# A planned encoder kernel: in-place steps counted at the shared port, other landing times, and six rank points for each stage

## The chip, the cores and the metric

The kernel runs on 1 core of one Trainium2 chip. The metric is device time in microseconds from launch to end, the median of 3 runs. The profile is one further execution of the same program; its span runs from the first to the last instruction.

## What is computed

A trunk of two layers on x of 1024 tokens by 1024 features, all in float32. Each layer does this (`lax` and reshapes left out):

```python
h = rms_norm(x, norm1_g[l])
proj = h @ w_in[l]
(a_cq, a_ckv, a_kr, b_q, b_k, b_v, c_q, c_k, c_v, d_q, d_k, d_v) = jnp.split(proj, splits, axis=-1)
y_a = mla_mixer(...)    # group A: latent attention, 4 heads, dense over 1024 keys
y_b = diff_mixer(...)   # group B: differential attention, 4 heads, two softmaxes each, dense
y_c = swa_mixer(...)    # group C: banded attention, +-128 tokens, sink logits
y_d = na_mixer(...)     # group D: neighbourhood attention on the 64-wide grid, with a bias
mix = jnp.concatenate([rms_norm(y_a, out_g_mla[l]), y_b,
                       rms_norm(y_c, out_g_swa[l]), rms_norm(y_d, out_g_na[l])], axis=-1)
x = x + mix @ w_out[l]
h = rms_norm(x, norm2_g[l])
x = x + jnp.square(jax.nn.relu(h @ w_up[l])) @ w_down[l]
```

and after the last layer a final `rms_norm`.

## The kernel before

The kernel is written as a program of steps, and the order of the steps is not the order of the code. Every call such as `nc.vector.tensor_tensor(...)` goes to `Plan.add`, which records a `Step`: its engine, its operands, and the steps that it must follow. `Plan.order`, the list pass, then walks through an imagined time, picks for each engine the ready step with the lowest rank, and gives tiles their buffers. `Trunk.emit` issues the steps in the order of their imagined starts. For that reason every instruction has the same line, L696, in the profile. On the chip each engine runs its own queue in that order, and engines wait for each other only where data or a buffer asks for it; the imagined times are not enforced.

What the pass knows of the chip stands in a few places:

- `Plan.price` gives each step an occupancy and a latency, from its engine and size. For a transfer it gives 470 ns for the issue on SyncE and a time that depends on the bytes and on the length of the contiguous runs.
- `Plan.issue` moves the imagined clock. A transfer begins some time after its issue and lands a fixed time after its last byte; a consumer gets a further `LATE`. A VectorE or GpSimd step with two wide inputs in SBUF takes the shared port: it starts no sooner than the last such step of either engine has ended. An input that is the same view as the output is not in `s.ins` and so does not count as an input there.
- `s.slack` belongs to TensorE's steps. In the first of two searches a step is passed over until it has been ready for `slack` ns; only where nothing else can go does the second search take it. Matmuls and transposes that read `p` (probabilities) have a slack of their own, with another value in stage `b`.
- `SPAN` gives each stage of each layer a list of points ("knots"). `Plan.stream` spreads the stage's steps evenly over the list by TensorE cost, and the rank of a step is read off between two points. A stage whose points are lower goes first wherever both are ready. A step's rank is also lowered to that of any step that needs it.
- `Place.ROOM` caps the live buffers of each tile name; a name that is not in it has the count in the code (`bufs`, or `CAPS` by stage).

The stages of a layer: `open` (norm, first three column tiles of the input projection, and the first rotary tables), `b1`, `lat`, `pd`, `pc` (the other projections), `up` (the latent products of group A), `b`, `d`, `c`, `a` (attention by group), `mb`, `md`, `mc`, `ma` (norm and gain of the groups' outputs, split in a high and a low part, the tiles `mix`), `o1`, `o2` (output projection), and `mlp`. Attention stages overlap freely; MLP is a Strassen-like product with 16 groups of up-projection and 4 of down-projection.

Steps and tiles named below: matrix products run as three passes of fp32r parts, so operands are split: ScalarE makes the high part, VectorE or GpSimd subtracts it for the low part (`xh`/`xl`, `wh`/`wl`, `both`, `mix`). `sq` and `acc` are sums of squares, added in place. `tabc` and `tabs` are rotary tables, multiplied in place by a row of norms. `yc` and `y` are the outputs of groups, multiplied in place by `rz`, the inverse denominators. `raw` are MLP weights, combined by additions and subtractions, partly in place (`s1`, a sum of two, has two buffers in the code). `lat`, `qb`, `kb` are DRAM tensors that the kernel writes and reads back, into `latp` and `stack`. `act` are MLP activations read back. In an in-place call the code passes the same view twice:

```python
def times(self, y, rz, eng=None):
    self.tt(y, y, rz, eng=eng or self.nc.gpsimd)
```

All transfers but 96 stores of the MLP are issued by SyncE, in the planned order; a transfer whose data or buffer is not ready holds up those behind it.

Of the kernel before, what the change touches and what calls it, by code (L numbers as in the profile page):

```python
# [249 lines left out]

class Step:
    __slots__ = ("n", "eng", "op", "args", "kw", "outs", "ins", "before", "after", "rank", "unit",
                 "start", "done", "cells", "cost", "tiled", "slack")


class Unit:
# [16 lines left out]
class Plan:  # L273
# [42 lines left out]
    def add(self, q, op, args, kw):  # L316
        s = Step()
        s.n, s.eng, s.op, s.args, s.kw = len(self.steps), q, op, args, kw
        out = kw.get("out", args[0] if args else None)
        s.outs = [v for v in (out, kw.get("accum_out")) if isinstance(v, View)]  # L320
        s.ins = [v for v in chain(args, kw.values()) if isinstance(v, View) and all(v is not o for o in s.outs)]
        s.rank = self.lead
        s.unit = self.unit or Unit()
        s.unit.steps.append(s)
        s.start, s.tiled = None, False
        before = set()

        def clash(a, b):
            if not np.may_share_memory(a, b):
                return False  # L330
            if a.ndim == b.ndim == 2 and a.strides == b.strides and a.strides[1] == 4 < a.strides[0]:
                row, wide = divmod(b.ctypes.data - a.ctypes.data, a.strides[0])
                hits = lambda r, c: -b.shape[0] < r < a.shape[0] and -4 * b.shape[1] < c < 4 * a.shape[1]
                return hits(row, wide) or hits(row + 1, wide - a.strides[0])
            try:
                return np.shares_memory(a, b, max_work=4000)
            except Exception:
                return True

        def same(a, b):  # L340
            return a.shape == b.shape and a.strides == b.strides and a.ctypes.data == b.ctypes.data

        for v in s.ins:
            c = v.cell
            before.update(p for p, a in c.writes if clash(a, v.arr))
            c.reads.append((s.n, v.arr))
        for v in s.outs:
            c, whole = v.cell, v.arr.size == v.cell.arr.size
            before.update(p for p, a in chain(c.writes, c.reads) if p != s.n and clash(a, v.arr))
            if whole:  # L350
                c.writes, c.reads = [], [r for r in c.reads if r[0] == s.n]
            else:
                c.writes = [w for w in c.writes if not same(w[1], v.arr)]
                c.reads = [r for r in c.reads if r[0] == s.n or not same(r[1], v.arr)]
            c.writes.append((s.n, v.arr))
        before.discard(s.n)
        s.before, s.after = [self.steps[p] for p in before], []
        for p in s.before:
            p.after.append(s)
        s.cells = []  # L360
        for v in chain(s.outs, s.ins):
            if v.cell.kind and v.cell not in s.cells:
                s.cells.append(v.cell)
        for c in s.cells:
            c.steps.append(s)
        s.cost = self.price(s)
        s.slack = 0
        if q.name == "tensor":
            names = {v.cell.name for v in s.ins}
            s.slack = (1996 if self.stage == "b" else 248) if "p" in names else 0 if names & self.FIRM else 1996  # L370
            if names & {"rs_r", "rz", "sq", "part"} and self.stage not in ("open", "b1"):
                s.slack = 2087
        self.steps.append(s)
        return s


    def price(self, s):

        q, op = s.eng.name, s.op
        out = s.outs[0] if s.outs else None  # L380
        if op == "dma_start":
            runs = []
            for v in s.args[:2]:
                if isinstance(v, View):
                    dims = [(st // 4, n) for st, n in zip(v.arr.strides, v.arr.shape)]
                else:
                    dims = list(v.ap)
                run = 1
                for st, n in reversed(dims):
                    if n > 1:  # L390
                        if st != run:
                            break
                        run *= n
                if isinstance(v, View) and v.cell.kind and run > v.arr.shape[-1]:
                    run = min(run, math.prod(v.cell.shape[1:]))
                runs.append(run)
            size, run = 4 * max(v.arr.size for v in s.args[:2] if isinstance(v, View)), min(4 * min(runs), 4096)
            per = 12 + run / 26.5 if run >= 512 else 9 + run / 30
            return 470.0, size / run * per * 1.33 / 16
        n = math.prod(out.arr.shape[1:])  # L400
        psum = any(v.cell.kind == "bank" for v in s.ins)
        if q == "tensor":
# [10 lines left out]
        if q == "scalar":  # L413
            d = 0.832 * n + (50 if psum else 94)
# [7 lines left out]
        d = 1.04 * n + 65  # L422
# [110 lines left out]

    LOOK, HOLD = 40, {}
    FIRM = {"wh", "wl", "wah", "wal", "wkeep", "stack", "v"}
    LATE = 537

    def stuck(self, avail):
        lines = []
# [45 lines left out]
    def issue(self, s, t):  # L585

        q = s.eng.name
        s.start = t
        occ, lat = s.cost
        if s.op == "dma_start":  # L590
            lane = self.turn % 8
            self.turn += 1
            t = s.start = max(t, self.lanes[lane])
            begin = max(t + 1100, self.pipe)
            self.pipe = begin + lat
            s.done = self.pipe + (100 if any(v.cell.kind for v in s.ins) else 950)
            self.lanes[lane] = s.done + 17
            return t + occ
        if q == "tensor":
            k = int(t // 3413.33)  # L600
            while self.window < k:
                self.window += 1
                was, a = self.slow[self.window - 1], self.act.get(self.window - 1, 0.0) / 3413.33
# [9 lines left out]
            s.done = t + occ * (2 if s.tiled else 1) + 180 * (1.5 if slow else 1)  # L613
            return t + occ
        if q in ("vector", "gpsimd"):
            wide = [v for v in s.ins if math.prod(v.arr.shape[1:]) > 1]
            if len(wide) > 1 and all(v.cell.kind != "bank" for v in wide):
                t = max(t, self.port)
                self.port = t + occ
                s.start = t  # L620
# [4 lines left out]
class Place:  # L625


    def __init__(self, plan, bufs=1):
# [2 lines left out]
    CAPS = {"st": {"b": 10, "d": 8, "c": 6, "a": 12}, "p": {"b": 5, "d": 4, "c": 4, "a": 6},  # L631
            "v": {"b": 2, "d": 2, "c": 2, "a": 3}, "pt": {"b": 6, "d": 6, "c": 6, "a": 8},
            "y": {"b": 2, "d": 2, "c": 2, "a": 2}}
    ROOM = {'a4': 13, 'act10': 15, 'bias3': 2, 'big16': 19, 'cb4': 10, 'es4': 3, 'mask1': 3, 'ms2': 7,
# [5 lines left out]

    def tile(self, shape, dt, tag, bufs=None, name=None):
        n, bufs, stage = math.prod(shape[1:]), bufs or self.bufs, self.plan.stage
# [13 lines left out]
class Trunk:  # L656
# [264 lines left out]
    def attention(self, l):  # L921
# [162 lines left out]
                share(self.mm_ps(), m, 1, self.weights(w_out[m, 0]) + self.weights(w_out[m, 1]), range(8))  # L1084

    SPAN = {
        'open': ((20.62, 20.78, 85.68, 85.85), (1310.39, 1339.46, 1345.64, 1356.83)),
        'b1': ((83.39, 102.03, 186.33, 225.41), (1317.52, 1397.09, 1531.38, 1531.38)),
        'lat': ((274.83, 295.08, 308.49, 326.42), (1506.09, 1506.09, 1570.31, 1573.33)),
# [13 lines left out]
        'mlp': ((618.60, 841.24, 1010.20, 1261.11), (1855.54, 2022.97, 2217.58, 2430.52)),}  # L1103
    SOON, IDLE = 20, 12
    BANKS = {"mm": 8, "tr": 4, "sb": 2, "pv": 2}
    EARLY, NP = 4, 6
# [992 lines left out]
```

## Time and profile before

| | |
|---|---|
| median of 3 runs | 2492.53 us (2492.34 to 2497.19) |
| the profiled execution | 2490.28 us, span 2488.5 us |
| TensorE busy (matmuls) | 2445.0 us, 98% |
| VectorE busy | 1894.0 us, 76% |
| ScalarE busy | 1294.0 us, 52% |
| GpSimd busy | 379.8 us, 15% |
| mean granted TensorE clock | 0.996 |
| moved by DMA | 378.31 MB, mean 152 GB/s |

PE is TensorE, PEld its weight loads, DVE VectorE, ACT ScalarE, POOL GpSimd, SP SyncE. In rows of instructions `out<-in` names tiles, and x is the count. A row of stretches has start and end, length, the busy time of each engine with its count of instructions, then the granted TensorE clock (1.00 is full), the share of the DMA engines that is busy, and GB/s. Idle time of TensorE in a stretch is its length less PE's busy time. In the chain (the work that ended last, followed back from the end) a row is start, length, and what it is.

### The profile page before, as it was taken

The page shows a single profiled execution, that of the slowest core. Times are in us where ns is not written, and L with a number is a line of the kernel's source. Part 1 is how long each engine was busy: PE and PEld are TensorE (multiplying, and loading weights), DVE is VectorE, ACT ScalarE, POOL GpSimd, SP SyncE. Part 2 cuts the span into 40 slices and gives each one's busy share as a digit, 9 for nine tenths or more (in the row PEclk, how much of TensorE's full clock was granted, in tenths as well). Part 3 has the DMA queues.
Part 4 walks back from the last instruction along what each step waited for, and adds up shares of the span by engine and source line. Part 5 has one row for each costly group of instructions (what it writes and reads, how often), then busy time and mean ns, then how long its engine had stood idle before and what let it go on. Part 6 is the DMA issues. An engine that isn't in the chain of part 4 may idle for free.

```text
span 2488.5 us, 35364 instructions
## 1 busy us (share of the span) xinstructions
PE 2445.0 (98%) x12260; PEld 1962.3 (79%) x12260; DVE 1894.0 (76%) x3536; ACT 1294.0 (52%) x2405; POOL 379.8 (15%) x266
## 2 busy tenths in 40 slices
PE   8999999999999999999999999999999999999998
PEld 6777776777888888888877777777788888888887
DVE  7588757767877779888657786777688777897886
ACT  4466656644544445444426565676555444544454
POOL 4033324113000000000032241330330000000000
PEclk9999999999999999999999999999999999999999
DMA  5455487522244468444143645874313444774321
GB/s 188 135 165 140 124 253 231 157 83 75 98 151 154 151 219 286 137 148 144 72 140 100 176 136 144 222 235 126 109 58 127 157 150 164 248 246 153 122 89 68
DMA packets 207220, 378.31 MB, mean 152 GB/s; under 512 B 40817, under 2 KB 55361, under 8 KB 207041
## 3 DMA queue, kind: packets, MB, share of 16 engines
q1 hardware_dynamic: 192064, 349.83, 45.0%
q10 hardware_dynamic: 14976, 26.22, 2.7%
q8 instruction: 97, 1.59, 0.3%
q14 instruction: 83, 0.67, 0.1%
HBM read 259.89 MB, written 116.07 MB: 151 GB/s over the span
## 4 chain that ended last, share of the span: by engine, by line
PE 86%; DVE 6%; DMA 2%; issue 2%; ACT 2%; SPq 1%; POOL 1%; DVEq 0%; POOLq 0%; ACTq 0%
PE bank L696 86%; DVE p L696 2%; DVE part L696 1%; SPq L696 1%; ACT p L696 1%; DMA lat<-both 1%; DMA ws<-in_w_in 1%; DVE mix L696 1%; DVE sq L696 0%; DVE xl L696 0%; DVE x L696 0%; DVE raw L696 0%; DVE both L696 0%; DVE col L696 0%; POOL wl L696 0%
## 5 line engine op out<-in xcount | busy, mean ns | idle before, releaser
L696 PE MATMUL bank<-far,wh 128*128 128x512 f32 (+1 forms) x2848 | 869.4, 387 | 0.0
L696 PEld LDWEIGHTS bank<-far,wh 128*128 128x128 f32 x2848 | 532.3, 188 | 108.6 <-ACT ev L696 0.4
L696 PE MATMUL bank<-far,wl 128*128 128x512 f32 (+1 forms) x1424 | 550.2, 387 | 0.0
L696 ACT ACTIVATE p<-p,col 128x1024 f32<-128x1024 f32 (+2 forms) x320 | 294.4, 921 | 142.1 <-DVE col L696 136.8
L696 POOL TENSOR_TENSOR wl<-ws,wh 128x512 fp32r<-128x512 f32 (+1 forms) x122 | 166.1, 1366 | 1078.3 <-DVE xl L696 611.5
L696 PEld LDWEIGHTS bank<-far,wl 128*128 128x128 f32 x1424 | 267.4, 188 | 54.5
L696 PE MATMUL bank<-stack 96*128 96x512 f32 (+2 forms) x896 | 282.7, 395 | 5.1 <-ACT pt L696 1.5
L696 PE MATMUL bank<-ident,p 128*128 128x128 f32 x1376 | 237.7, 275 | 7.4 <-DVE col L696 6.5
L696 DVE TENSOR_TENSOR x<-bank,x 128x512 f32<-128x512 f32 (+1 forms) x276 | 187.6, 680 | 55.0 <-PE bank L696 54.2
L696 PEld LDWEIGHTS bank<-ident,p 128*128 128x128 f32 x1376 | 173.0, 142 | 50.7 <-DVE col L696 8.9
L696 PE MATMUL bank<-xh,wh 128*128 128x512 f32 x480 | 196.7, 413 | 3.2 <-ACT wh L696 2.1
L696 PE MATMUL bank<-xl,wh 128*128 128x512 f32 x480 | 195.6, 412 | 1.9 <-DVE xl L696 1.9
L696 PE MATMUL bank<-xh,wl 128*128 128x512 f32 x480 | 193.3, 410 | 0.7 <-POOL wl L696 0.7
L696 PEld LDWEIGHTS bank<-stack 96*128 96x128 f32 (+1 forms) x896 | 158.5, 189 | 44.2 <-issue 11.1
L696 ACT ACTIVATE pt<-bank 128x512 f32<-128x512 f32 (+2 forms) x256 | 136.5, 558 | 102.2 <-PE bank L696 99.7
L696 DVE CUSTOM_DVE_ANT_0 p<-bank,zero 128x512 f32<-128x512 f32 x192 | 131.4, 684 | 66.2 <-PE bank L696 62.7
L696 PE MATMUL bank<-pt,v 128*64 128x256 f32 (+2 forms) x1344 | 170.6, 391 | 0.5 <-ACT pt L696 0.5
L696 DVE CUSTOM_DVE_ANT_0 p<-bank,zero,col 128x512 f32<-128x512 f32 x192 | 143.6, 748 | 34.9 <-PE bank L696 21.9
L696 DVE TENSOR_TENSOR wl<-raw,wh 128x512 fp32r<-128x512 f32 x224 | 153.0, 686 | 15.1 <-ACT wh L696 14.9
L696 PE MATMUL bank<-mix,wh 128*128 128x512 f32 x512 | 160.2, 393 | 2.6 <-DVE mix L696 2.6
L696 ACT ACTIVATE ev<-ev 128x512 f32<-128x512 f32 x128 | 80.6, 632 | 150.4 <-DVE ev L696 149.6
L696 DVE TENSOR_TENSOR far<-act,far 128x512 fp32r<-128x512 f32 x224 | 148.2, 688 | 0.8 <-ACT far L696 0.6
(169 smaller groups left out, 4030.6 us busy)
## 6 DMA issues: line engine op xcount, KB each, us to landing
act<-acts SPq DMA_DIRECT2D x224, 256.0 KB
raw<-in_w_up SPq DMA_DIRECT2D x128, 256.0 KB
acts<-ev SPq DMA_DIRECT2D x128, 256.0 KB
acts<-ev ACTq DMA_DIRECT2D x96, 256.0 KB
c<-in_w_down SPq DMA_DIRECT2D x64, 256.0 KB
ws<-in_w_in SPq DMA_DIRECT2D x60, 256.0 KB
rz<-drows SPq DMA_DIRECT2D x40, 256.0 KB
ws<-in_w_out SPq DMA_DIRECT2D x40, 256.0 KB
```

The source lines that it names most:

```text
L696: getattr(s.eng.engine, s.op)(*[real(a) for a in s.args], **{k: real(a) for k, a in s.kw.items()})
```

## The change

The change is in what the list pass believes and in its numbers; no step of the computation is added or removed.

- Whether a VectorE or GpSimd step takes the shared port is now found when it is recorded, from `in0` and `in1`. So a step whose output is also one of its two inputs counts as well.
- The transfer's price, its landing time, which now depends on direction and run length, and `LATE` are other numbers.
- The slacks of TensorE's steps are other numbers.
- `ROOM` has other caps. Some names drop out of it and so fall back to the counts in the code: `s12` had 7, and has the 2 of the code.
- `SPAN` has six points instead of four for each stage and layer of attention; `mlp` keeps four. All values differ.

```diff
@@ Step
-                 "start", "done", "cells", "cost", "tiled", "slack")
+                 "start", "done", "cells", "cost", "tiled", "slack", "port", "land")
@@ Plan.add
         s.cost = self.price(s)
+        wide = [v for v in (kw.get("in0"), kw.get("in1")) if v is not None and math.prod(v.arr.shape[1:]) > 1]
+        s.port = (q.name in ("vector", "gpsimd") and len(wide) > 1
+                  and all(v.cell.kind != "bank" for v in wide))
         s.slack = 0
         if q.name == "tensor":
             names = {v.cell.name for v in s.ins}
-            s.slack = (1996 if self.stage == "b" else 248) if "p" in names else 0 if names & self.FIRM else 1996
+            s.slack = (459 if self.stage == "b" else 1337) if "p" in names else 0 if names & self.FIRM else 459
             if names & {"rs_r", "rz", "sq", "part"} and self.stage not in ("open", "b1"):
-                s.slack = 2087
+                s.slack = 2014
@@ Plan.price, for a transfer
-            per = 12 + run / 26.5 if run >= 512 else 9 + run / 30
-            return 470.0, size / run * per * 1.33 / 16
+            stored = any(v.cell.kind for v in s.ins)
+            s.land = 180 + 2200 * (run < 300) if stored else 750 + 1320 * (run >= 3000 and bool(s.ins))
+            per = run / 20.7 if run >= 512 else 19.6 + run / 28.3
+            return 470.0, size / run * per / 16
@@ Plan
-    LATE = 537
+    LATE = 1096
@@ Plan.issue
-            begin = max(t + 1100, self.pipe)
+            begin = max(t + 1140, self.pipe)
             self.pipe = begin + lat
-            s.done = self.pipe + (100 if any(v.cell.kind for v in s.ins) else 950)
+            s.done = self.pipe + s.land
...
         if q in ("vector", "gpsimd"):
-            wide = [v for v in s.ins if math.prod(v.arr.shape[1:]) > 1]
-            if len(wide) > 1 and all(v.cell.kind != "bank" for v in wide):
+            if s.port:
                 t = max(t, self.port)
@@ Place.ROOM
-    ROOM = {'a4': 13, 'act10': 15, 'bias3': 2, 'big16': 19, 'cb4': 10, 'es4': 3, 'mask1': 3, 'ms2': 7,
...
+    ROOM = {'a4': 17, 'act10': 37, 'b4': 5, 'bias3': 9, 'big16': 18, 'c4': 9, 'cb4': 8, 'es4': 1, 'mask1': 18,
...
@@ Trunk.SPAN
-        'open': ((20.62, 20.78, 85.68, 85.85), (1310.39, 1339.46, 1345.64, 1356.83)),
-        'b1': ((83.39, 102.03, 186.33, 225.41), (1317.52, 1397.09, 1531.38, 1531.38)),
...
+        'open': ((4.74, 4.96, 16.89, 18.35, 19.82, 19.95), (1235.16, 1277.84, 1352.73, 1352.88, 1354.75, 1354.86)),
+        'b1': ((44.40, 115.65, 125.33, 194.32, 206.17, 210.57), (1255.80, 1342.65, 1362.89, 1548.02, 1723.38, 1735.54)),
...
-        'mlp': ((618.60, 841.24, 1010.20, 1261.11), (1855.54, 2022.97, 2217.58, 2430.52)),}
+        'mlp': ((634.22, 854.14, 1028.40, 1268.26), (1892.26, 1997.85, 2238.58, 2446.95)),}
```

More of the change, by code (lines that the diff above doesn't have):

```diff
@@ L1086 @@
     SPAN = {
-        'open': ((20.62, 20.78, 85.68, 85.85), (1310.39, 1339.46, 1345.64, 1356.83)),
-        'b1': ((83.39, 102.03, 186.33, 225.41), (1317.52, 1397.09, 1531.38, 1531.38)),
-        'lat': ((274.83, 295.08, 308.49, 326.42), (1506.09, 1506.09, 1570.31, 1573.33)),
[13 rows of a table removed]
-        'mlp': ((618.60, 841.24, 1010.20, 1261.11), (1855.54, 2022.97, 2217.58, 2430.52)),}
+        'open': ((4.74, 4.96, 16.89, 18.35, 19.82, 19.95), (1235.16, 1277.84, 1352.73, 1352.88, 1354.75, 1354.86)),
+        'b1': ((44.40, 115.65, 125.33, 194.32, 206.17, 210.57), (1255.80, 1342.65, 1362.89, 1548.02, 1723.38, 1735.54)),
+        'lat': ((251.45, 270.52, 310.02, 313.34, 318.06, 318.72), (1508.86, 1508.86, 1530.37, 1538.37, 1565.71, 1574.40)),
[13 rows of a table added]
+        'mlp': ((634.22, 854.14, 1028.40, 1268.26), (1892.26, 1997.85, 2238.58, 2446.95)),}
     SOON, IDLE = 20, 12
```

36 rows, old and new, of tables (ROOM, SPAN) are left out of this document.

## The prediction

> **What bounds the kernel.** I read the page first (span and busy times, then the chain that ended last), then the busy time by stretch, and last the order of time of VectorE and GpSimd where TensorE is idle.
>
> ```profile
> span 2488.5 us, 35364 instructions
> PE 2445.0 (98%) x12260; PEld 1962.3 (79%) x12260; DVE 1894.0 (76%) x3536; ACT 1294.0 (52%) x2405; POOL 379.8 (15%) x266
> ```
>
> ```profile
> PE 86%; DVE 6%; DMA 2%; issue 2%; ACT 2%; SPq 1%; POOL 1%; DVEq 0%; POOLq 0%; ACTq 0%
> ```
>
> TensorE is busy for 2445.0 of 2488.5 us and is 86% of the chain. No matmul is added or taken away, so a plan can win only from the 43.5 us in which TensorE is idle, and from slow stretches behind them. The stretches below (start and end, length, busy time of each engine, granted clock, DMA share, GB/s) show where those are.
>
> ```profile
> 0.00:60.00 60.00, 53.17 (x223) 41.69 (x224) 43.44 (x60) 30.27 (x45) 25.82 (x21) 0.97 0.53 188
> 60.00:350.00 290.00, 287.18 (x1573) 220.81 (x1572) 203.23 (x500) 169.94 (x325) 77.14 (x55) 1.00 0.56 158
> 350.00:400.00 50.00, 45.38 (x260) 33.73 (x258) 43.14 (x105) 34.29 (x95) 23.82 (x16) 0.97 0.65 186
> 400.00:563.00 163.00, 161.38 (x1041) 122.84 (x1040) 114.09 (x250) 101.99 (x196) 40.43 (x25) 1.00 0.51 156
> 563.00:1236.00 673.00, 672.68 (x2977) 557.19 (x2978) 535.87 (x838) 308.03 (x530) 23.96 (x20) 1.00 0.44 148
> 1236.00:1300.00 64.00, 59.50 (x273) 48.03 (x273) 40.29 (x47) 21.38 (x34) 25.07 (x14) 1.00 0.57 171
> 1300.00:1546.00 246.00, 242.52 (x1311) 187.99 (x1309) 182.33 (x428) 142.98 (x269) 70.83 (x53) 1.00 0.44 129
> 1546.00:1625.00 79.00, 72.47 (x445) 54.28 (x443) 58.31 (x149) 50.30 (x128) 25.86 (x17) 1.00 0.80 221
> 1625.00:1783.00 158.00, 156.62 (x1032) 118.80 (x1030) 113.70 (x269) 107.66 (x214) 39.83 (x25) 1.00 0.58 171
> 1783.00:2466.00 683.00, 682.47 (x3052) 565.86 (x3053) 542.76 (x854) 319.52 (x557) 27.05 (x22) 1.00 0.42 140
> 2466.00:2488.00 22.00, 11.68 (x90) 11.11 (x89) 16.80 (x47) 7.66 (x20) 0.00 (x0) 0.77 0.53 192
> ```
>
> The two MLP stretches (563 to 1236, 1783 to 2466) leave 0.32 and 0.53 us idle. Their matmuls come every 672.68/2977 = 0.226 us: nothing can be won in 1356 us of the span. The last 22 us (10.3 idle) are the final norm, which stays last whatever the ranks. What is left is attention: 6.83 and 4.50 us idle in the two openings, 4.62 and 6.53 us in the stretches where the latent products meet the groups D and C, and 2.82, 1.62, 3.48 and 1.38 us in the four long ones.
>
> **The change, part by part.** The program's steps stay; their order on each engine's queue, the buffers they get, and the order of DMA issues on SyncE change with the numbers of the list pass.
>
> *Part 1, in-place steps hold the port.* Before, a two-input step whose output is also an input was not held apart. These rows show what that lets through: fine stretches, then steps of the two engines in order of time (start, length), two pieces of the chain, and a group (busy, mean ns, idle before).
>
> ```profile
> 40.00:46.00 6.00, 4.82 (x22) 3.63 (x20) 5.94 (x6) 0.00 (x0) 5.42 (x3) 1.00 0.00 1
> 375.00:380.00 5.00, 3.54 (x21) 2.09 (x19) 5.00 (x3) 2.74 (x7) 5.00 (x3) 1.00 0.53 144
> 380.00:385.00 5.00, 2.71 (x14) 2.72 (x14) 4.57 (x11) 1.79 (x5) 0.54 (x1) 0.70 1.04 234
> 560.00:565.00 5.00, 3.22 (x13) 2.41 (x13) 4.86 (x7) 2.69 (x7) 2.71 (x2) 0.79 0.18 52
> 1250.00:1255.00 5.00, 3.13 (x14) 2.27 (x13) 5.00 (x3) 0.38 (x1) 5.00 (x4) 1.00 0.74 276
> ```
>
> ```profile
> 24.75 1.21 DVE L696 TENSOR_TENSOR sq<-sq 128x1024 f32<-128x1024 f32 x1
> ...
> 40.33 1.72 DVE L696 TENSOR_TENSOR tabc<-tabc,rb 128x1024 f32<-128x1024 f32 x1
> 41.97 2.31 DVE L696 TENSOR_TENSOR tabs<-tabs,rb 128x1024 f32<-128x1024 f32 x1
> ...
> 374.24 7.51 DVE L696 SCALAR_TENSOR_TENSOR mix<-rz,g_sub,mix 128x512 fp32r<-128x512 f32 x4 [2.32 <-ACT mix L696]
> 374.96 2.84 POOL L696 TENSOR_TENSOR tabc<-tabc,rq 128x1024 f32<-128x1024 f32 x1
> 555.87 5.17 POOL L696 TENSOR_TENSOR yc<-yc,rz 128x1024 f32<-128x1024 f32 x2 [1.31 <-DMA rz<-drows]
> 1758.99 1.40 DVE L696 SCALAR_TENSOR_TENSOR mix<-y,par,mix 128x512 fp32r<-128x512 f32 x2
> ```
>
> ```profile
> 555.32 0.70 DVE raw L696
> ...
> 556.04 2.77 DVE raw L696
> ...
> 1249.07 2.31 DVE sq L696
> ```
>
> ```profile
> L696 DVE SCALAR_TENSOR_TENSOR xl<-x,par,xh 128x1024 fp32r<-128x1024 f32 x15 | 21.9, 1471 | 3.1 <-ACT xh L696 3.1
> ```
>
> At 374.24 four `mix` steps take 7.51 us; two like them take 1.40, so four should take 2.80. They run beside GpSimd's in-place `tabc`. TensorE is idle for 1.46 + 2.29 = 3.75 us between 375 and 385, and its granted clock then falls to 0.70, another 0.30 x 5 = 1.5 us at most: 5.25. At 556 a `raw` step takes 2.77 instead of 0.70 beside the in-place `yc`; TensorE idles 1.78 us at 560 to 565 at a clock of 0.79 (0.21 x 5 = 1.05): 2.83. In the openings a 1024-wide step free of GpSimd takes 1.21 us. In layer 0 `tabc` and `tabs` lose 0.51 + 1.10 = 1.61 beside GpSimd (5.42 of 6 us busy), and TensorE idles 1.18 at 40 to 46: I count the smaller, 1.18. In layer 1 `sq` loses 1.10, where TensorE idles 1.87: 1.10. All of part 1 is thus 5.25 + 2.83 + 1.18 + 1.10 = 10.4 us. Its other end is not 0 but a loss: holding makes the plan let VectorE stand behind a 2.84 us GpSimd step that might have come later, so 2.84 at each of these four places, +11.4, is the upper end. How much of the 10.4 comes? The split `xl` is not in place; the old pass held it apart already, and its mean is still 1471 ns against 1.21 us for a free step of its width. Knowing of the port reduces collisions and does not end them. I take half, 5.2.
>
> The Trainium skill bears on this (SBUF — State Buffer, section Who interferes with whom): a VectorE instruction with two SBUF inputs contends with a GpSimd instruction that reads SBUF, and the one that starts first keeps the port to its end. The trace agrees: `yc` starts at 555.87 and `raw`, from 556.04, takes 2.77. The page adds "Issue order, not op shape, decides who blocks", and that speaks against the change; by it alone part 1 would be 0 where the start order does not turn, and the sum below 3.3 instead of 8.5.
>
> *Part 2, landing times and `LATE`.* Pieces of the chain, and the longest wait of SyncE's queue (total, times, longest):
>
> ```profile
> 1292.02 2.92 DMA stack<-kb
> ...
> 1599.96 6.38 DMA lat<-both
> 1608.14 5.08 DMA latp<-lat
> ```
>
> ```profile
> SPq L696 <- DVE wl L696: 227.9, 67, 37.6
> ```
>
> For the 128 KB `stack<-kb` the old constants give 1100 + 443 + 950 + 537 = 3.03 us, the new 1140 + 396 + 2070 + 1096 = 4.70, against 2.92 on the chip: now on the safe side. For the 512 KB `latp<-lat` it is 4.36 before and 5.89 after, against 5.08. Consumers are ordered later behind other ready work, which costs an engine nothing while such work is there, and loads keep their place behind the steps that SyncE waits for in order (37.6 us at the longest behind one `wl`). The place where it counts is 1546 to 1625, where `lat` and `latp` stand on the chain and 6.53 us are idle. Between 0 and 6.53 I take half, 3.3. The mirror is a loss of the same size if a load slides behind such a wait.
>
> *Part 3, slack of TensorE.* Transposes of probabilities in stage b are held back for 459 ns instead of 1996, elsewhere for 1337 instead of 248.
>
> ```profile
> PE bank L696 <- DVE col L696: 12.6, 11, 3.7
> ```
>
> TensorE waits 11 times, 12.6 us, for the row minimum or scale on the way to a transpose. More slack outside b can take some away, less in b can add some. Between -12.6 and +12.6 (as many again) I take 0, since the two edits pull apart.
>
> *Part 4, `ROOM` and six rank points.* These decide who overtakes whom. In the MLP the cap of `s1` falls from 7 to its own 2 and `act` rises to 37; I cost that at nothing, because VectorE, which fills `s1`, is free for 137 of 673 us there and TensorE idles 0.32. If the cover went, one 0.70 us VectorE step would show in each of 2 x 16 groups, +22 us. In attention the new ranks can as well close the long stretches' gaps (2.82 + 1.62 + 3.48 + 1.38 = 9.3 us) as double them; I take 0.
>
> Sum: -5.2 - 3.3 = -8.5 us on the profiled execution's own 2490.28 us (span 2488.5), so 2481.8. The median of the runs shown, 2492.53, stands 2.25 above that execution; measured as the runs are, 2484 us.
>
> **The rivals.**
>
> *Nothing measurable* (2492 us, with 2487.5 to 2497.5). The pass orders each queue, and no semaphore is added between VectorE and GpSimd. When one drifts by a microsecond the same steps meet again, at these or other places. Part 1 at 0 leaves -3.3, 2489.2 us on the same scale, and a like loss from the new ranks gives 2492. For it: `xl`, above. Against: two of the collisions, at 374 and 556, come from steps of 2.8 and 5.2 us, and a drift of a microsecond does not bring those together again.
>
> *Slower* (2504 us). The place is stage b, 60 to 350 and 1300 to 1546, now with 6.3 us idle for 2884 matmuls. With 459 ns of slack a transpose goes to TensorE's in-order queue soon after its exponential, and when VectorE is late (203.23 of 290 us busy there) every matmul behind it waits too, at 12.6/11 = 1.15 us each. Eight such waits (9.2 us) eat the gain; from 12 on (13.8) it is slower by over 0.2%; 18 give 20.7 - 8.5 = +12.2, some 2504 us. Against it: 6.3 us shows that stage b has other work in plenty.
>
> *Much faster* (2467.5 us). All idle time of attention except the first opening closes: 2.82 + 4.62 + 1.62 + 4.50 + 3.48 + 6.53 + 1.38 = 25 us. For it: the six rank points act on every stretch. Against: the last few tenths of each stretch are changes between transposes, products and weight loads.
>
> **How the numbers follow.** Forecast, 2477 to 2487.5 us: 0.38. Much faster, below 2477: 0.19. Nothing measurable: 0.21. Slower: 0.22. About 0.2%, 5 us, is what a measurement of this kernel can tell from no change. Faster is 0.38 + 0.19 = 0.57. The range runs from just below the much faster case, 2465, to just short of the slower one, 2503; it leaves about 0.1 out on each side. The forecast alone has 2477 to 2487.5.
>
> **What would show it.** Part 1 right: no stretched `mix` or `raw` next to `tabc` or `yc`, and clock windows of 1.00 there; TensorE's idle time down by about 6 us in the openings and at the ends of attention. Part 2: less idle time in layer 1's latent stretch. Part 3: the wait for `col` stays near 12.6 us. Part 4: MLP stretches still within 1 us of full. The forecast is wrong if TensorE's idle time outside these places grows, above all in stage b, or if the MLP shows gaps.

## The result, and the profile after

The changed kernel takes 2450.3 us (median of 4 runs, 2449.2 to 2454.87) against 2493.28 us (median of 4 runs too, 2492.34 to 2497.19); the ratio is 0.983 (95% interval 0.981 to 0.985). That is 43 us, where 8.5 were forecast, and it lies below the range of 2465 to 2503. The next fence has two lines of the page after.

```profile
span 2447.4 us, 35378 instructions
PE 2429.7 (99%) x12260; PEld 1963.4 (80%) x12260; DVE 1881.9 (77%) x3536; ACT 1297.4 (53%) x2405; POOL 377.5 (15%) x266
```

The span is 41.1 us shorter. TensorE's idle time went from 43.5 to 17.7 us, and its busy time fell by 15.3 us with the same 12260 matmuls. So more was to be had than the idle time, from which the prediction had started. Stretches of the profile after, cut at about the same places of the program as those of before (columns as there):

```profile
0.00:60.00 60.00, 56.85 (x252) 45.76 (x253) 46.13 (x54) 29.21 (x43) 34.69 (x24) 1.00 0.56 197
60.00:350.00 290.00, 289.74 (x1607) 226.00 (x1607) 217.62 (x529) 176.38 (x340) 77.33 (x58) 1.00 0.58 165
350.00:400.00 50.00, 48.65 (x336) 39.19 (x334) 38.31 (x112) 42.85 (x125) 22.78 (x15) 1.00 0.86 230
400.00:549.00 149.00, 148.02 (x922) 112.65 (x919) 95.89 (x216) 85.87 (x153) 33.59 (x23) 0.99 0.51 151
549.00:1219.00 670.00, 670.00 (x2974) 555.49 (x2973) 544.61 (x847) 317.50 (x537) 26.65 (x20) 1.00 0.44 148
1219.00:1283.00 64.00, 63.84 (x298) 53.14 (x297) 32.25 (x37) 16.55 (x27) 18.49 (x11) 1.00 0.48 148
1283.00:1525.00 242.00, 241.65 (x1324) 186.62 (x1322) 185.03 (x433) 145.14 (x273) 74.22 (x54) 1.00 0.49 144
1525.00:1600.00 75.00, 73.69 (x481) 58.00 (x481) 62.50 (x171) 57.93 (x151) 34.27 (x24) 1.00 0.82 235
1600.00:1752.00 152.00, 151.67 (x990) 116.24 (x985) 102.24 (x238) 97.43 (x187) 34.82 (x24) 1.00 0.54 166
1752.00:2425.00 673.00, 673.00 (x3001) 558.33 (x3002) 539.89 (x856) 319.91 (x551) 20.61 (x16) 1.00 0.42 140
2425.00:2447.00 22.00, 12.54 (x99) 11.97 (x97) 17.39 (x49) 8.63 (x22) 0.00 (x0) 0.82 0.53 192
```

The opening of layer 1 has 0.16 us idle instead of 4.50, the latent stretches 1.35 and 1.31 instead of 4.62 and 6.53, the four long stretches of attention together 1.92 instead of 9.30. The MLP is full, as before: from its first to its last product with `far` it takes 602.0 and 604.9 us in the two layers of before, and 601.9 and 604.9 us after. All but some 1 us of the gain lies ahead of these products, in attention and its hand-over to the MLP.

Where busy time fell shows in the groups of TensorE (busy, mean ns of one, idle before). First three groups of before, then the same of after:

```profile
L696 PE MATMUL bank<-ident,p 128*128 128x128 f32 x1376 | 237.7, 275 | 7.4 <-DVE col L696 6.5 <-DVE part L696 0.4 <-ACT p L696 0.2
L696 PE MATMUL bank<-xh,wh 128*128 128x512 f32 x480 | 196.7, 413 | 3.2 <-ACT wh L696 2.1 <-ACT xh L696 0.7 <-DVE col L696 0.5
L696 PE MATMUL bank<-xl,wh 128*128 128x512 f32 x480 | 195.6, 412 | 1.9 <-DVE xl L696 1.9
```

```profile
L700 PE MATMUL bank<-ident,p 128*128 128x128 f32 x1376 | 232.8, 274 | 2.6 <-DVE col L700 1.2 <-DVE part L700 1.1
L700 PE MATMUL bank<-xh,wh 128*128 128x512 f32 x480 | 192.4, 406 | 1.3 <-ACT xh L700 1.3
L700 PE MATMUL bank<-xl,wh 128*128 128x512 f32 x480 | 191.0, 406 | 0.0
```

These three lose 4.9 + 4.3 + 4.6 = 13.8 us of busy time. A row of a matmul of 512 columns lasts about 0.39 us, but in the MLP one starts every 0.226 us: up to some 0.16 us of waiting between two starts lies under the row before it and counts as busy. Less of this, and less time at half clock (382.0 to 385.4 us of before, for one, are at 0.50), can shorten busy time. The mean granted clock is 0.998, it was 0.996: 0.004 of 2488.5 us less 0.002 of 2447.4, an estimate of some 5 us. The other 10 us or so of the 15.3 would then be waiting that no idle time shows; this split is an estimate.

### The profile page after: what moved, and what is told of

Its sections match the earlier page's. It is cut to its first block, busy times and chain, and to the rows that moved or that the text cites. A ratio compares the mean times of both kernels' runs of the same rounds, so it can differ in the third digit from the quotient of the medians.

```text
span 2447.4 us, 35378 instructions
## 1 busy us (share of the span) xinstructions
PE 2429.7 (99%) x12260; PEld 1963.4 (80%) x12260; DVE 1881.9 (77%) x3536; ACT 1297.4 (53%) x2405; POOL 377.5 (15%) x266
## 4 chain that ended last, share of the span: by engine, by line
PE 93%; DVE 3%; DMA 2%; ACT 1%; issue 1%; SPq 0%; POOL 0%; DVEq 0%; ACTq 0%; POOLq 0%
PE bank L700 93%; DVE p L700 1%; DVE x L700 1%; DMA latp<-lat 0%; DVE part L700 0%; DVE col L700 0%; DMA ws<-in_w_lat 0%; SPq L700 0%; DVE ev L700 0%; DMA va<-part 0%; DMA x<-in_x 0%; ACT p L700 0%; DVE sq L700 0%; DMA qar<-both 0%; DMA qan<-both 0%
## 5 line engine op out<-in xcount | busy, mean ns | idle before, releaser
L700 PE MATMUL bank<-ident,p 128*128 128x128 f32 x1376 | 232.8, 274 | 2.6 <-DVE col L700 1.2
L700 PEld LDWEIGHTS bank<-ident,p 128*128 128x128 f32 x1376 | 172.0, 141 | 43.5 <-issue 5.3
L700 ACT ACTIVATE wh<-raw 128x512 fp32r<-128x512 f32 x224 | 136.3, 622 | 80.5 <-DVE raw L700 55.3
```

What stands on the lines that cost most here:

```text
L700: getattr(s.eng.engine, s.op)(*[real(a) for a in s.args], **{k: real(a) for k, a in s.kw.items()})
```

## The experiments

Each was timed in 3 rounds beside the kernel before, which stood at 2492.7 to 2494.6 us in these comparisons. The names of the five parts are: port (in-place steps count), transfers (price, landing time and `LATE`), slacks, caps (`ROOM`), ranks (`SPAN`). Three theories: **M**, the truer beliefs (port and transfers) carry the gain; **N**, the numbers (ranks above all) carry it; **F**, all of it was fitted together, and any edit spoils one exact order.

### One part undone

Four kernels are the changed one with one part as before. The edits, in the order of the texts that follow:

```diff
-            if s.port:
+            wide = [v for v in s.ins if math.prod(v.arr.shape[1:]) > 1]
+            if len(wide) > 1 and all(v.cell.kind != "bank" for v in wide):
```
```diff
-    LATE = 1096
+    LATE = 537      # and the old price, start and landing time of a transfer
```
```diff
-        'open': ((4.74, 4.96, 16.89, 18.35, 19.82, 19.95), ...
+        'open': ((20.62, 20.78, 85.68, 85.85), ...              # all rows of SPAN as before
```
```diff
-    ROOM = {'a4': 17, 'act10': 37, ...
+    ROOM = {'a4': 13, 'act10': 15, ...                          # all caps as before
```

> The changed kernel with the old rule for the shared port (an in-place step does not count), all other numbers new. Theory M (the truer beliefs of the list pass carry the gain): some 10 us of the 43 come back, 2460, with stretched in-place steps beside GpSimd on TensorE's path again. Theory N (the new ranks carry it): within 5 us of the changed kernel, 2450 to 2455. Theory F (beliefs and numbers fit only each other, any part undone spoils the order): over 20 us slower than the changed kernel, 2470 or more.

> The changed kernel with the old transfer prices, landing times and LATE. Theory M: 10 to 15 us come back, 2460 to 2465, with waits of TensorE or VectorE for lat, latp, stack. Theory N: within 5 us of the changed kernel. Theory F: 2470 or more.

> The changed kernel with the old four rank points for each stage and layer. Theory M: most of the gain stays, 2460 or less. Theory N: most of it goes, 2480 to 2493, with the first output projection matmul again at about 530 us instead of 411. Theory F: 2480 or more too, and possibly slower than the kernel before.

> The changed kernel with the old caps of live buffers. Theories M and N with ranks alone: within 5 us of the changed kernel. N with the caps as a part: 10 us or more slower. Theory F: 2470 or more.

| undone | time, us | ratio to the kernel before | slower than the changed kernel by |
|---|---|---|---|
| port | 2456.7 | 0.985 (0.983 to 0.987) | 6 |
| transfers | 2468.9 | 0.990 (0.988 to 0.992) | 19 |
| ranks | 2478.1 | 0.994 (0.992 to 0.996) | 28 |
| caps | 2482.7 | 0.996 (0.994 to 0.997) | 32 |

The four sum to 85 us, twice the gain. Neither M nor N alone fits: undone ranks cost much, as in N, but undone caps cost more. The 6 us of the port are not clear of noise: their interval, 0.983 to 0.987, meets that of the changed kernel, 0.981 to 0.985.

### Beliefs alone, numbers alone, and moved points

```diff
 # beliefs: the kernel before with s.port and the new transfers; numbers: with the new slacks, ROOM and SPAN
 # after_jitter, before_jitter: every number of SPAN moved at random by up to 2.0, each list sorted again, e.g.
-        'open': ((4.74, 4.96, 16.89, 18.35, 19.82, 19.95), (1235.16, ...
+        'open': ((3.28, 6.35, 17.37, 17.95, 19.75, 19.80), (1235.77, ...
```

> The kernel before with the new port rule and the new transfer prices, landing times and LATE; ranks, caps and slacks are the old ones. Theory M: most of the gain of 43 us, 2460 or less. Theory N: no change, 2488 to 2498. Theory F (beliefs and numbers fit only each other): slower than the kernel before, 2500 or more, since the old numbers now meet beliefs they were not made for.

> The kernel before with the new ranks, caps and slacks; port rule and transfers are the old ones. Theory M: little, 2485 or more. Theory N: most of the gain, 2460 or less. Theory F: 2475 or more, since undoing the beliefs singly cost 6 and 19 us, at least 25 together.

> The changed kernel with each rank point moved by a random amount of up to 2.0 either way (and sorted again). Theories M and N, where the order is good for a reason that one can name (stage overlap, no collisions): within 5 us of the changed kernel, 2450 to 2455. Theory F: the gain hangs on the exact points, 2460 or more.

> The kernel before with its four rank points moved in the same way. It gives the scatter of any such edit: theories M and N 2488 to 2500. Theory F: the old points were fitted to the old beliefs too, so 2500 or more.

Beliefs alone: 2478.6 us, ratio 0.993 (0.992 to 0.995), 16 us of gain. Numbers alone: 2469.8, ratio 0.990 (0.988 to 0.991), 25 us. The two sum to 41 of the 43 us: each half works without the other, which F denied. But the moved points of the changed kernel take 2468.1, ratio 0.989 (0.987 to 0.991), 18 us more than the exact ones; and those of the kernel before 2498.1, ratio 1.001 (1.000 to 1.002). So F is right on one thing: 18 of the 43 us hang on the exact points of the changed kernel.

### Each belief alone, one row of ranks, and a small move

```diff
 # port_alone, transfers_alone: the kernel before with that part; a_late: the kernel before with one row of SPAN:
-        'a': ((460.00, 473.91, 475.50, 475.50), (1655.67, 1673.44, 1711.80, 1779.68)),
+        'a': ((979.07, 984.15, 1040.07, 1192.60, 1221.93, 1223.61), (1644.95, 1693.71, 1694.58, 1714.67, 1839.28, 1890.40)),
```

> The kernel before with the new port rule alone. The two beliefs together gave -15.4 us (2478.6). Theory P (the port rule gives what the prediction priced it at, half of 10.4): 2488 to 2491, the stretched mix and raw steps beside tabc and yc gone from TensorE's path. Theory T (the transfers carry the beliefs' part): within 3 us of the kernel before.

> The kernel before with the new transfer prices, landing times and LATE alone. Theory T: 2478 to 2484. Theory P: 2488 or more. As in the prediction (half of the 6.53 us of one stretch): 2490, with the latent stretch of layer 1 shorter and all else the same.

> The kernel before with one row of ranks from the changed kernel: stage a (group A's attention) has points far behind those of the output projection instead of ahead of them, so that it is drawn forward only by what needs it. Theory O (the overlap of the output projection's first half with group A's attention fills TensorE and is what the ranks bring): first output projection matmul at some 420 to 450 us instead of 534, and 2475 to 2485. Theory F (single numbers bring nothing without the rest): early matmuls or not, 2490 or more.

> The changed kernel with each rank point moved by up to 0.2 instead of 2.0, another draw. Theory F (the exact points): still 2460 or more, since any move of a step past another changes all that follows. A smooth dependence on the points: a tenth of the 18 us of the larger move, 2452.

Port alone: 2477.2 us, ratio 0.993 (0.991 to 0.994), a gain of 15.9, three times the 5.2 that it was priced at. Transfers alone: 2488.8, ratio 0.998 (0.997 to 0.999), a gain of 4.3, where 3.3 had been taken; but added to the port rule (2477.2 us, then 2478.6 with both) they gain nothing. The row `a` alone: 2499.1, ratio 1.002 (1.001 to 1.003); in that kernel the output projection did not start early either (538 us), so it does not try theory O. The move by 0.2 costs as much as that by 2.0: 2466.8, ratio 0.988 (0.986 to 0.990). The dependence on the points is not smooth.

What did the port rule do to the collisions? Four groups of VectorE, of before and of port alone:

```profile
L696 DVE TENSOR_TENSOR raw<-raw 128x512 f32<-128x512 f32 x128 | 96.3, 752 | 7.2 <-POOL wl L696 4.5
L696 DVE SCALAR_TENSOR_TENSOR p<-p,col 128x1024 f32<-128x1024 f32 x64 | 91.1, 1424 | 1.1
L696 DVE TENSOR_TENSOR sq<-sq 128x1024 f32<-128x1024 f32 x20 | 29.3, 1466 | 1.1 <-ACT sq L696 1.1
L696 DVE SCALAR_TENSOR_TENSOR mix<-rz,g_sub,mix 128x512 fp32r<-128x512 f32 x8 | 10.7, 1378 | 2.3 <-ACT mix L696 2.3
```

```profile
L698 DVE TENSOR_TENSOR raw<-raw 128x512 f32<-128x512 f32 x128 | 95.6, 747 | 7.4 <-POOL wl L698 4.7
L698 DVE SCALAR_TENSOR_TENSOR p<-p,col 128x1024 f32<-128x1024 f32 x64 | 94.3, 1474 | 1.2
L698 DVE TENSOR_TENSOR sq<-sq 128x1024 f32<-128x1024 f32 x20 | 30.3, 1513 | 1.4 <-ACT sq L698 1.1
L698 DVE SCALAR_TENSOR_TENSOR mix<-rz,g_sub,mix 128x512 fp32r<-128x512 f32 x8 | 10.6, 1353 | 1.7 <-ACT mix L698 1.6
```

The steps are stretched as much as before, `p` and `sq` a little more. The longest `raw` still takes 2.76 us and the longest `mix` 2.88 (2.76 and 2.87 before). Counted over all two-input steps of VectorE, 78 of before and 75 of port alone are over 0.15 us longer than the quick ones of their form, 65 and 62 us too long in all, and each of them overlaps a step of GpSimd. But TensorE does not wait for them as long (its longest waits in port alone, in the view of waits: total, times, longest):

```profile
PE bank L698 <- DVE part L698: 4.5, 3, 2.0
PE bank L698 <- DMA stack<-kb: 3.9, 2, 2.1
PE bank L698 <- DVE col L698: 3.2, 5, 2.2
```

The wait for `col` is 3.2 us where it was 12.6. The rule brought its gain with the collisions still there. The idle time in layer 1's latent stretch, where the prediction placed the worth of the transfers, goes with this rule too: from 1530 to 1630 us TensorE idles 6.5 us before, 5.5 with the transfers alone and 3.1 with the port alone.

### The parts at points that nobody chose for them

To tell a part's worth from the loss of one exact order, three kernels have the points of after_jitter (2468.1 us) with one part undone, edited as in the first group, and one has the points of before_jitter (2498.1 us) with the port rule added.

> The points of after_jitter (2468.1 us), with the old port rule. Theory R (each part has a worth of its own at any points): the port rule was worth 15.9 alone, so 2475 to 2485. Theory F (an edit only throws away one exact order, which the moved points have thrown away already): within 4 us of 2468.

> The points of after_jitter (2468.1 us), with the old transfer prices, landing times and LATE. Theory R: 2472 to 2487 (worth 4.3 alone, 18.6 when undone). Theory F: within 4 us of 2468.

> The points of after_jitter (2468.1 us), with the old caps of live buffers. Theory R: 32 us when undone at the exact points, 17 of which any edit costs, so some 2483. Theory F: within 4 us of 2468.

> The points of before_jitter (2498.1 us), with the new port rule alone. Theory R: the rule brings its 15.9 us here too, 2478 to 2486. Theory F: the 15.9 were one lucky order; here within 5 us of 2498.

| undone at the moved points | time, us | ratio to the kernel before | slower than after_jitter by |
|---|---|---|---|
| port | 2487.9 | 0.998 (0.996 to 0.999) | 20 |
| transfers | 2481.2 | 0.995 (0.993 to 0.996) | 13 |
| caps | 2509.9 | 1.007 (1.005 to 1.008) | 42 |

The port rule added at the points of before_jitter: 2479.3, ratio 0.994 (0.992 to 0.995), 19 us faster than before_jitter. Theory F falls: no part is without effect at moved points. But theory R, a worth of its own for each part at any points, does not hold either: for the caps it gave 2483, 27 us too little. The kernels above and in this table form six pairs that differ by the port rule alone:

| port rule added to | without, us | with, us | gain, us |
|---|---|---|---|
| the kernel before | 2493.1 | 2477.2 | 16 |
| the kernel before with the new transfers | 2488.8 | 2478.6 | 10 |
| before_jitter | 2498.1 | 2479.3 | 19 |
| new numbers, old transfers | 2469.8 | 2468.9 | 1 |
| new numbers, new transfers | 2456.7 | 2450.3 | 6 |
| new numbers moved, new transfers | 2487.9 | 2468.1 | 20 |

With the old numbers the rule brings 10 to 19 us. With the new ones it brings 20 at the moved points and at the exact points little that is clear of noise. The wait for `col` does not explain this in general: from before_jitter to the kernel with the rule it goes from 6.9 to 3.5 us, and with the new numbers moved from 5.9 to 4.3.

Ranks and caps can be crossed in the same way. All of these kernels have both new beliefs; the first has the old slacks too:

| | old caps | new caps |
|---|---|---|
| old ranks | 2478.6 (beliefs) | 2478.1 (ranks undone) |
| new ranks | 2482.7 (caps undone) | 2450.3 (the changed kernel) |
| new ranks, moved | 2509.9 | 2468.1 |

The new caps (with the new slacks) bring 0.5 us to the old ranks, the new ranks bring nothing to the old caps, and both together bring 28 us, or 10 at the moved points. So 32 and 42 us are not what the caps are worth: they are what it costs to run the new ranks in the old caps. Ranks and caps fit each other.

Where the caps and the transfers act is seen in stretches. After_jitter, the start of the program and the hand-over from attention to the MLP in both layers:

```profile
0.00:60.00 60.00, 58.10 (x255) 46.62 (x256) 46.61 (x58) 29.77 (x44) 32.05 (x23) 1.00 0.56 197
...
549.00:640.00 91.00, 88.55 (x387) 72.01 (x387) 70.10 (x100) 47.16 (x84) 24.72 (x18) 1.00 0.18 53
1750.00:1830.00 80.00, 78.03 (x344) 63.25 (x343) 53.92 (x71) 34.55 (x61) 30.68 (x23) 0.98 0.25 74
```

The same hand-overs with the old caps (the second is 30 us later there):

```profile
549.00:640.00 91.00, 84.40 (x356) 67.60 (x355) 58.81 (x73) 37.84 (x67) 32.05 (x24) 0.92 0.21 60
1780.00:1860.00 80.00, 67.78 (x294) 53.18 (x293) 44.92 (x59) 29.12 (x52) 24.38 (x20) 0.89 0.21 64
```

Idle time is 6.6 and 12.2 us instead of 2.5 and 2.0, and the granted clock is 0.92 and 0.89, where it was 1.00 and 0.98: another 0.08 x 91 + 0.09 x 80 = 14.5 us of lost clock at most, beside 14.3 us of idle time. Most of the caps' price (29 of the 46 us between the two profiled executions, at most) lies where the output projection ends and the MLP begins. With the old transfers the start of the program is the worst place:

```profile
0.00:60.00 60.00, 54.58 (x224) 44.27 (x225) 42.47 (x56) 28.96 (x43) 29.95 (x21) 0.91 0.54 193
```

There 5.4 us are idle instead of 1.9, at a clock of 0.91: up to 5.4 us of clock beside 3.5 us of idle time, of a total of 13.

### Slacks, and the early output projection

Both kernels have the points of after_jitter.

```diff
 # no_slack_moved
-            s.slack = (459 if self.stage == "b" else 1337) if "p" in names else 0 if names & self.FIRM else 459
+            s.slack = (1996 if self.stage == "b" else 248) if "p" in names else 0 if names & self.FIRM else 1996
 # and 2014 back to 2087; late_rows_moved: the rows a, mb, md, mc, ma, o1 and o2 of SPAN as before (and moved), mlp moved by another draw
```

> The points of after_jitter (2468.1 us), with the old slacks of TensorE's steps. As the prediction took it (the two edits pull apart, 0): within 5 us of 2468. If the slacks matter by themselves: 2478 or more, with more waits of TensorE for col.

> The points of after_jitter, but stages a, mb, md, mc, ma, o1 and o2 have the old four points (moved by up to 2.0 too). Theory O (the early output projection fills TensorE beside group A's attention and is what the ranks bring): first output projection matmul near 520 us, and 2480 or more (28 us when all ranks were undone, 17 of which any edit costs, leaves some 11). Without O: within 5 us of 2468.

The old slacks: 2478.9 us, ratio 0.994 (0.993 to 0.996), 11 us slower; TensorE waits for `col` 8 times, 6.6 us, where it was 6 times, 4.3. Late rows: 2458.7, ratio 0.987 (0.985 to 0.988), 9 us faster than after_jitter. Here are the output projection's matmuls (ns shortest/median/longest, first and last start) in the changed kernel, in after_jitter, and then with late rows:

```profile
L700 PE MATMUL bank<-mix,wh x512: 387/389/632, 410.8 to 1818.8; 128*128 128x512 f32 x171
```

```profile
L700 PE MATMUL bank<-mix,wh x512: 387/389/797, 416.8 to 1837.2; 128*128 128x512 f32 x171
```

```profile
L700 PE MATMUL bank<-mix,wh x512: 387/389/499, 517.2 to 1824.4; 128*128 128x512 f32 x171
```

With late rows the first is at 517 us instead of 417 in after_jitter, and the kernel is no slower than after_jitter for it. Theory O falls, as far as one draw can show: the plainest difference between the two orders is not what the ranks bring. By what steps the ranks bring their part, and only with the new caps, was not found. With all ranks undone 28 us are lost, 17 of which small moves cost as well.

## Why the prediction was wrong

**What it had right.** The direction; that attention alone can win (the MLP stayed full); that the tail would hardly move (9.5 us idle, it was 10.3). The transfers, taken at 3.3, were worth 4.3 alone, but this is luck: the sum had them beside the port rule, where they bring nothing, and half of the idle time in their place went with the port rule alone. Two of the four places named in part 1 were cleared in the changed kernel, but so they were with the port rule undone. First the changed kernel, then the one without the rule:

```profile
L700 DVE TENSOR_TENSOR raw<-raw 128x512 f32<-128x512 f32 x128 | 87.6, 685 | 0.1
L700 DVE SCALAR_TENSOR_TENSOR mix<-rz,g_sub,mix 128x512 fp32r<-128x512 f32 x8 | 6.2, 801 | 0.1
```

```profile
L698 DVE TENSOR_TENSOR raw<-raw 128x512 f32<-128x512 f32 x128 | 87.4, 684 | 0.1
L698 DVE SCALAR_TENSOR_TENSOR mix<-rz,g_sub,mix 128x512 fp32r<-128x512 f32 x8 | 5.8, 738 | 0.0
```

The longest `raw` and `mix` take 0.69 and 1.20 us in the first, 0.69 and 0.75 in the second. The new numbers parted these steps from `yc` and `tabc`; the rule, which was to do it, left them at 2.76 and 2.88 us when it stood alone.

**Part 1, the term of 5.2, measured 16 on the kernel before.** The step that failed is "Knowing of the port reduces collisions and does not end them. I take half". It priced the rule by the collisions it would remove, at four places. The port alone removed hardly any (75 stretched steps, it was 78) and still won 15.9 us. The quoted rule of the Trainium skill (SBUF — State Buffer, section Who interferes with whom), that issue order decides who blocks, was not contradicted: the blocked steps stayed. The inference from it, no turned order and so no gain, was wrong. That the pass now gives late steps their real place and puts other work before what waits for them is a reading that would fit; it was not tried by itself, and the shorter wait for `col` supports it on the kernel before only, not in the two other settings looked at. How the rule wins stays open.

**Parts 3 and 4, the terms taken at 0.** The steps that failed are "I take 0" on the new ranks and "I cost that at nothing" on the caps. Ranks, caps and slacks won 25 us without the beliefs and 28 on top of them. Where edits pull both ways I took the middle of a wide interval, and priced each part by itself. By themselves the 0 was about right: new caps at old ranks bring 0.5 us, new ranks in old caps lose 4. What the sum had no term for is the two together. The step on caps looked only inside the MLP (`s1`, 0.32 us idle); with the new ranks, old caps cost most at the hand-over into it, which the prediction did not name. The 0 on slacks failed too: the old ones cost 11 us at the moved points.

**The bound.** "A plan can win only from the 43.5 us in which TensorE is idle, and from slow stretches behind them" was used with the first half only: the much faster rival was the sum of idle times, 25 us, and set the lower end of the range at 2465. The kernel won 25.8 us of idle time and 15.3 us of busy time. The Trainium skill warns of this (Perfetto Trace Analysis, section Identifying the Most-Contended Engine): the share of time that matmuls are busy does not tell well how close a kernel is to the roofline, because pipelined instructions look smaller in the trace. The traces agree that busy time misleads, with 15.3 us, but not on the sign: here the rows look longer than the step from start to start (0.389 against 0.226 us). The rival nearest to the result was "much faster", given 0.19; its time, 2467.5, was 17 us too high.

**The slower rival.** Less slack in stage b did not bring the waits: in the changed kernel TensorE waits 5 times for `col`, 4.7 us in all, where it was 11 times, 12.6. The sign given for part 3, a wait that stays near 12.6, did not come true either.

```profile
PE bank L700 <- DVE col L700: 4.7, 5, 2.2
```

**What stays open.** Some 17 us of the gain belong to the exact points: moves by 0.2 and by 2.0 lose them alike, late rows lose 8. Which steps that are passed make this difference was not found. The parts at 11 and 13 us are one draw each, and single draws differ by about 9 us (late_rows_moved and after_jitter), so these two sizes are rough, and so are the 1 and 6 of the port at the exact points. The 16 to 20 of the port in three settings stand clear of that, and so do the 28 of ranks and caps together, though 18 of them belong to the exact points. Caps without the new slacks at the old ranks, and caps alone on the kernel before, were not run.

## What to carry to other kernels

A change to a list pass is priced badly by the places where engines collide: here a truer belief on the port won 10 to 19 us with the old numbers while the collisions stayed. When the bound engine's rows are longer than the step from one start to the next, its idle time understates what can be won; compare start-to-start times with those of a full stretch. And try a part in several settings, and parts in pairs, before crediting any: the port rule here looked like 1, 6, 10, 16, 19 or 20 us, and new ranks and new caps, each worth nothing without the other, won 28 together.

## What the runs showed that I had not expected

A move of rank points by 0.2, some 0.01% of the range that they span, changed the time by 16.5 us, as much as a move ten times as large (17.8). And TensorE's granted clock takes part in such prices: with the old caps it fell to 0.92 and 0.89 at the two hand-overs, where 2.5 and 2.0 us of idle time had become 6.6 and 12.2.
